# Branch gate a's weight units spread between those of queries and recurrence input; gates kept as sums, their tanh taken in place beside gate b

## The chip, the cores and the metric

The kernel runs on one core of a Trainium2 chip. The metric is the device time of one launch in microseconds (us). TensorE multiplies matrices out of SBUF into PSUM, VectorE (DVE) and ScalarE (ACT) work on tiles of 128 partitions, and SyncE (SP) issues nearly all the transfers from HBM. Each engine works through its own instructions in the order that the program fixed; engines wait for one another through semaphores.

## The reference

One layer over a sequence of 256 positions of width 2048, one core, float32:

```python
h = _modulate(_rms_norm(x, norm1_g), shift1, scale1)
proj = jnp.einsum("bsd,de->bse", h, w_in)
lru_x, lru_gate, q, k, v, g_a, g_b = jnp.split(proj, split_idx, axis=-1)
rec = _rg_lru(causal_conv(lru_x), ...)
y_a = (rec * gelu(lru_gate)) @ w_lru_out
y_b = _swa_sink_attention(q, k, v, ...) @ w_attn_out
merged = sigmoid(g_a) * y_a + sigmoid(g_b) * y_b
x = x + gate1 * (merged @ w_out)
x = x + gate2 * (relu(h2 @ w_ff1) ** 2 @ w_ff2)      # h2 from the second norm
```

The six vectors shift1 to gate2 are `silu(c) @ w_ada + b_ada`. The sigmoids of both branch gates are computed as tanh of half the argument; the 1 that belongs to it is added where the gate is multiplied, and a half later on.

## The kernel before

Everything is kept transposed: 128 features on the partitions, 256 positions in a row. A block of 128 output features is called f. The input projection has 84 blocks: 2 of keys, 2 of values, 16 of queries, 16 of recurrence input (`lx`), 16 of the gelu gate (`lg`), 16 of gate a (`F_GA`), 16 of gate b (`F_GB`).

Each weight and each activation is split into a high part and a rest, and three products are summed. For weights ScalarE writes the high part `wh` (L161) and DVE the rest `wl` (L163), 1024 columns at a time, each with four buffers (`WH_BUFS`). The raw weights come into four buffers of 1 MB (`RAW_BUFS`), which the loads of `w_ada` use too: `ada_unit` loads 1 MB and DVE multiplies it with the broadcast condition and sums it up (L287, 96 times in all). This text calls that a wada sum.

Work is cut into units of one weight load each. A wide unit (`gemm_wide`) has all 16 row blocks of one f: 32 matmuls, 2 splits of 1024 columns on each engine, and at the end ScalarE copies one half of the PSUM tile out (L197) and DVE adds the other half (L198). The blocks up to f = 55 were begun in earlier passes; their remaining row blocks make narrow units (`gemm`): two f of 6 row blocks each (1536 weight columns) for keys to the first four gelu gates, one f of 10 row blocks (1280 columns) for the other gelu gates and the first four blocks of gate a. So gate a has 4 narrow units and 12 wide ones, gate b 16 wide ones.

The list `units` sets the order: keys, values, 8 units of queries, 8 of recurrence input, 14 of the gelu gate, 16 of gate a, 16 of gate b, and then 48 wide units for the projections of the two branches and of the merged branches (`ya_unit`, `yb_unit`, `out_unit`), and the MLP. Behind each unit a credit, in proportion to its columns, takes steps from the list `side` that earlier units put there with `later`: attention scores and values, the recurrence (convolution L566 and L568, gates L576 to L582, decay, scan), the gelu. A second credit issues wada sums. A scheduler then settles each engine's order. `ya_unit(0)` first splits the 16 recurrence outputs into high part and rest (L146, L147).

Activation functions that need a table loaded into ScalarE go through `table`, which keeps functions of one table together; the tanh of the branch gates (L637, L640) before the change does not go through it.

Of the kernel before, what the change touches and what calls it, by code (L numbers as in the profile page):

```python
# [12 lines left out]
AF = mybir.ActivationFunctionType  # L13
# [13 lines left out]
F_K, F_V, F_Q, F_LX, F_LG, F_GA, F_GB = 0, 2, 4, 20, 36, 52, 68  # L27
# [31 lines left out]
def hybrid_layer(ctx: ExitStack, tc: tile.TileContext, x, xt, wada, w_p, w_r, w_f, vec, lruw, relb,  # L59
# [19 lines left out]
    def pair(dt=F32):  # L79
        return kp.tile([P, 2, T], dt, tag="k2", name=nm("k"))  # L80
# [101 lines left out]
    def gemm_wide(parts, acts, join=True, out=None):  # L182

        ps = pg.tile([P, 2, T], F32, tag="pg", name=nm("pg"))
        n = len(acts)
        for k, hl in enumerate(acts):
            wh, wl = parts[k * P // WCH]
            w = slice(k * P % WCH, k * P % WCH + P)
            if k > 0:
                te.matmul(ps[:, 0], lhsT=wl[:, w], rhs=hl[:, 0], start=False, stop=False)  # L190
            te.matmul(ps, lhsT=wh[:, w], rhs=hl, start=k == 0, stop=k == n - 1)  # L191
            if k == 0:
                te.matmul(ps[:, 0], lhsT=wl[:, w], rhs=hl[:, 0], start=False, stop=False)  # L193
        if not join:
            return ps
        t = tmp([P, T]) if out is None else out
        se.activation(t, ps[:, 1], AF.Copy)  # L197
        ve.tensor_tensor(out=t, in0=ps[:, 0], in1=t, op=ALU.add)  # L198
        return t
# [91 lines left out]
    h = [None] * KT  # L291
# [71 lines left out]
    res = {}  # L363
# [45 lines left out]
    def add_unit(run, src=None, n=2048, native=False):  # L409
        if src is None:  # L410
            src = w_f[full[0]]
            full[0] += 1
        units.append((run, src, n, native))

    def later(cost, fn, *a):
        side.append((cost, fn, a))

    def in_unit(f, fin, nf=1):

        kd = _done(f)  # L420
        if kd:
            n = (KT - kd) * nf * P
            src = w_r[w_off[0]:w_off[0] + n * P].rearrange("(p n) -> p n", p=P)
            w_off[0] += n * P

            def run(w):
                for i in range(nf):
                    o = i * (KT - kd)
                    ps = gemm_native(w, o, kd, KT) if f in NATIVE_REST else gemm(w, o, h[kd:])
                    fin(f + i, ps, res[f + i])  # L430
            add_unit(run, src, n, f in NATIVE_REST)
        else:
            add_unit(lambda w: fin(f, gemm_wide(w, h), None))

    def in_units(f0, n, fin):
        f = f0
        while f < f0 + n:
            nf = 2 if f + 1 < f0 + n and _done(f) == _done(f + 1) and _done(f) >= KT // 2 else 1
            in_unit(f, lambda f, ps, part: fin(f - f0, ps, part), nf)
            f += nf  # L440
# [186 lines left out]
        ve.tensor_tensor(out=part, in0=ps, in1=part, op=ALU.add)  # L627
        later(1.6, lru_gelu, j)

    bg = [None]  # L630

    def branch_gate(f, ps, part):
        if part is None:
            if f % 2 == 0:
                bg[0] = pair()
            res[f] = bg[0][:, f % 2]
            se.activation(res[f], ps, AF.Tanh, scale=0.5)  # L637
        else:
            ve.tensor_tensor(out=part, in0=ps, in1=part, op=ALU.add)
            se.activation(part, part, AF.Tanh, scale=0.5)  # L640


    att, mg = {}, {}
# [129 lines left out]
            ada_unit()  # L773


    in_units(F_K, 2, k_fin)
    in_units(F_V, 2, v_fin)
    in_units(F_Q, 16, q_fin)
    in_units(F_LX, 16, lx_fin)
    in_units(F_LG, 16, lg_fin)  # L780
    in_units(F_GA, 16, lambda f, ps, part: branch_gate(F_GA + f, ps, part))
    in_units(F_GB, 16, lambda f, ps, part: branch_gate(F_GB + f, ps, part))
    n_ya = len(units)
    n_z = n_ya + 32 + Z_FROM
    n_ff1 = n_ya + 48
# [152 lines left out]
```

## Time and profile before

| | |
|---|---|
| median of 3 runs | 1588.1 us (1587.84 to 1588.21) |
| the profiled execution | 1587.3 us, of which the span from the first to the last instruction is 1585.5 us |
| TensorE busy | 1546.4 us (98% of the span) |
| VectorE busy | 1217.3 us (77%) |
| ScalarE busy | 886.7 us (56%) |
| matmuls in the records | 9812 |

A profile shows one execution. Busy time is the union of the instructions' records on an engine; a wait is idle time before an instruction, put down to whatever released it last. PE is TensorE, PEld its weight loads. "L163" is line 163 of the kernel, `x16` a count, "PEclk" the granted clock of TensorE as a share of its upper level.

### The profile page before, as it was taken

The page shows a single profiled execution, that of the slowest core. Times are in us where ns is not written, and L with a number is a line of the kernel's source. Part 1 is how long each engine was busy: PE and PEld are TensorE (multiplying, and loading weights), DVE is VectorE, ACT ScalarE, POOL GpSimd, SP SyncE. Part 2 cuts the span into 40 slices and gives each one's busy share as a digit, 9 for nine tenths or more (in the row PEclk, how much of TensorE's full clock was granted, in tenths as well). Part 3 has the DMA queues.
Part 4 walks back from the last instruction along what each step waited for, and adds up shares of the span by engine and source line. Part 5 has one row for each costly group of instructions (what it writes and reads, how often), then busy time and mean ns, then how long its engine had stood idle before and what let it go on. Part 6 is the DMA issues. An engine that isn't in the chain of part 4 may idle for free.

```text
span 1585.5 us, 24919 instructions
## 1 busy us (share of the span) xinstructions
PE 1546.4 (98%) x9812; PEld 1385.7 (87%) x9812; DVE 1217.3 (77%) x1941; ACT 886.7 (56%) x1510; POOL 0.2 (0%) x4
## 2 busy tenths in 40 slices
PE   4999999999999999999999999999999999999997
PEld 3999998899988888888889988888888888888886
DVE  5898998898999878788898877965665556655664
ACT  5733447686796564445455863356434663356553
POOL 0000000000000000000000000000000000000000
PEclk6999999999999999999999999999999999999999
DMA  7998986556867768777886666965555555555551
GB/s 304 355 336 322 351 286 213 187 191 235 299 242 273 286 249 305 278 293 291 325 305 228 241 247 241 349 240 186 186 186 186 188 188 190 192 190 191 189 187 54
DMA packets 61125, 387.89 MB, mean 245 GB/s; under 512 B 6512, under 2 KB 10960, under 8 KB 18640
## 3 DMA queue, kind: packets, MB, share of 16 engines
q1 hardware_dynamic: 55728, 380.66, 66.2%
q10 hardware_dynamic: 5280, 5.64, 1.1%
q8 instruction: 77, 1.26, 0.3%
q14 instruction: 40, 0.33, 0.1%
HBM read 384.13 MB, written 2.15 MB: 244 GB/s over the span
## 4 chain that ended last, share of the span: by engine, by line
PE 90%; DVE 5%; issue 2%; ACT 2%; DMA 2%; ACTq 0%; DVEq 0%
PE pg L191 45%; PE pg L190 21%; PE pg L179 5%; PE pg L178 5%; PE pg L177 5%; PE pg L206 2%; DVE wl L163 2%; PE pg L193 1%; DMA ra<-in_wada_dram 1%; PE pg L726 1%; PE pg L727 1%; PE pg L728 1%; DVE t L500 1%; DVE t L527 1%; PE pa L532 1%
## 5 line engine op out<-in xcount | busy, mean ns | idle before, releaser
L191 PE MATMUL pg<-k,wh 128*128 128x512 f32 x3120 | 1078.0, 395 | 1.1 <-DVE k L147 1.1
L163 DVE TENSOR_TENSOR wl<-rw,wh 128x1024 fp32r<-128x1024 f32 (+2 forms) x534 | 627.2, 1179 | 267.4 <-ACT wh L161 261.2
L190 PE MATMUL pg<-k,wl 128*128 128x256 f32 x2925 | 818.1, 280 | 0.0
L161 ACT ACTIVATE wh<-rw 128x1024 fp32r<-128x1024 f32 (+2 forms) x534 | 541.1, 1020 | 493.2 <-PE pg L191 328.1
L191 PEld LDWEIGHTS pg<-k,wh 128*128 128x128 f32 x3120 | 572.2, 188 | 120.6 <-issue 1.4
L190 PEld LDWEIGHTS pg<-k,wl 128*128 128x128 f32 x2925 | 550.9, 188 | 9.5 <-ACT k L146 0.5
L177 PE MATMUL pg<-k,wh 128*128 128x256 f32 x832 | 238.1, 288 | 6.7 <-ACT k L146 6.5
L179 PE MATMUL pg<-k,wl 128*128 128x256 f32 x832 | 234.1, 284 | 4.1 <-DVE wl L163 4.1
L178 PE MATMUL pg<-k,wh 128*128 128x256 f32 x832 | 236.4, 285 | 0.1
L287 DVE CUSTOM_DVE_ANT_0 ra<-ra,scr,vc 128x2048 f32<-128x2048 f32 x96 | 225.1, 2346 | 11.7 <-DMA ra<-in_wada_dram 11.6
L177 PEld LDWEIGHTS pg<-k,wh 128*128 128x128 f32 x832 | 158.0, 190 | 9.7 <-ACT k L146 7.3
L179 PEld LDWEIGHTS pg<-k,wl 128*128 128x128 f32 x832 | 158.3, 191 | 5.6 <-DVE wl L163 5.3
L178 PEld LDWEIGHTS pg<-k,wh 128*128 128x128 f32 x832 | 158.7, 191 | 1.2 <-issue 0.5
L754 DVE SCALAR_TENSOR_TENSOR k<-pg,mod,k 128x256 f32<-128x256 f32 x128 | 61.9, 483 | 34.5 <-PE pg L191 32.4
L743 ACT ACTIVATE t<-t 128x256 f32<-128x256 f32 x55 | 23.0, 418 | 70.5 <-DVE t L198 70.4
L198 DVE TENSOR_TENSOR t<-pg,t 128x256 f32<-128x256 f32 x131 | 54.7, 418 | 0.3 <-ACT t L197 0.3
L193 PE MATMUL pg<-k,wl 128*128 128x256 f32 x195 | 54.5, 279 | 0.0
L197 ACT ACTIVATE t<-pg 128x256 f32<-128x256 f32 x131 | 48.0, 366 | 0.3 <-PE pg L191 0.3
L193 PEld LDWEIGHTS pg<-k,wl 128*128 128x128 f32 x195 | 36.7, 188 | 8.5
L727 PE MATMUL pg<-z,wh 128*128 128x256 f32 x144 | 41.0, 285 | 0.0
L728 PE MATMUL pg<-z,wl 128*128 128x258 f32 x144 | 40.8, 284 | 0.0
L726 PE MATMUL pg<-z,wh 128*128 128x258 f32 x144 | 40.8, 283 | 0.0
(161 smaller groups left out, 961.4 us busy)
## 6 DMA issues: line engine op xcount, KB each, us to landing
rw<-in_w_f_dram SPq DMA_DIRECT2D x204, 1024.0 KB, 4.9
ra<-in_wada_dram SPq DMA_DIRECT2D x96, 1024.0 KB, 6.3
rw<-in_w_p_dram SPq DMA_DIRECT2D x31, 1024.0 KB, 7.1
rw<-in_w_r_dram SPq DMA_DIRECT2D x20, 768.0 KB, 4.5
rw<-in_w_r_dram SPq DMA_DIRECT2D x16, 640.0 KB, 3.9
bt<-ud ACTq DMA_DIRECT2D x8, 512.0 KB, 3.8
lw<-in_lruw_dram SPq DMA_DIRECT2D x4, 512.0 KB, 5.0
k<-in_x_dram SPq DMA_DIRECT2D x8, 256.0 KB, 5.5
```

The lines of the kernel that those rows point to most:

```text
L161: pin(se.activation(wh[:, :c], raw[:, o:o + c], AF.Copy))
L163: pin(ve.tensor_tensor(out=wl[:, :c], in0=raw[:, o:o + c], in1=wh[:, :c].bitcast(F32), op=ALU.subtract))
L177: te.matmul(ps, lhsT=wh[:, w], rhs=hl[:, 0], start=k == 0, stop=False)
L178: te.matmul(ps, lhsT=wh[:, w], rhs=hl[:, 1], start=False, stop=False)
L179: te.matmul(ps, lhsT=wl[:, w], rhs=hl[:, 0], start=False, stop=k == n - 1)
L190: te.matmul(ps[:, 0], lhsT=wl[:, w], rhs=hl[:, 0], start=False, stop=False)
L191: te.matmul(ps, lhsT=wh[:, w], rhs=hl, start=k == 0, stop=k == n - 1)
L193: te.matmul(ps[:, 0], lhsT=wl[:, w], rhs=hl[:, 0], start=False, stop=False)
L287: pin(ve.tensor_tensor_reduce(out=raw, in0=raw, in1=scr, scale=1.0, scalar=vc[:, V_BADA + c:V_BADA + c + 1], op0=ALU.mult, op1=ALU.add, ac ...
L726: te.matmul(ps, lhsT=wh[:, e], rhs=z[k][:, 0:258], start=k == 0, stop=False)
L727: te.matmul(ps[:, 0:256], lhsT=wh[:, e], rhs=z[k][:, 258:514], start=False, stop=False)
L754: ve.scalar_tensor_tensor(out=x1[f], in0=ps[:, i], scalar=mod[:, 5 * KT + f:5 * KT + f + 1], in1=x1[f], op0=ALU.mult, op1=ALU.add)
```

## The change

`in_units` and `add_unit` still give each unit its part of the weight array, in the same order as before, so no address changes. The list of units is then put together in another order: keys and values, then the 16 units of queries and recurrence input with the 12 wide units of gate a spread among them (three behind every four), then the 14 gelu-gate units, the four narrow units of gate a, and gate b.

`gemm_wide` writes a gate's sum (L197, L198) straight into the tile in which the gate is kept (`gate_slot`) instead of into a temporary tile. The tanh is taken in place later: each unit of gate b puts two steps of 0.4 into `side`, one for the gate-a block of the same number and one for its own, and both now go through `table` with the exponential's table.

```diff
-            add_unit(lambda w: fin(f, gemm_wide(w, h), None))
+            add_unit(lambda w: fin(f, gemm_wide(w, h, out=gate_slot(f)), None))
...
+    bg = {}
+    def gate_slot(f):
+        if f // 2 not in bg:
+            bg[f // 2] = pair()
+        res[f] = bg[f // 2][:, f % 2]
+        return res[f]
+    def gate_tanh(f):
+        table("exp", se.activation(res[f], res[f], AF.Tanh, scale=0.5))
     def branch_gate(f, ps, part):
-        if part is None:
-            if f % 2 == 0:
-                bg[0] = pair()
-            res[f] = bg[0][:, f % 2]
-            se.activation(res[f], ps, AF.Tanh, scale=0.5)
-        else:
+        if part is not None:
             ve.tensor_tensor(out=part, in0=ps, in1=part, op=ALU.add)
-            se.activation(part, part, AF.Tanh, scale=0.5)
+        if f >= F_GB:
+            later(0.4, gate_tanh, f - F_GB + F_GA)
+            later(0.4, gate_tanh, f)
...
+    def of(f0, n, fin):
+        start = len(units)
+        in_units(f0, n, fin)
+        new = units[start:]
+        del units[start:]
+        return new
+    def spread(main, extra):
+        done = 0
+        for i, u in enumerate(main):
+            units.append(u)
+            while done < len(extra) * (i + 1) // len(main):
+                units.append(extra[done])
+                done += 1
+    u_k, u_v = of(F_K, 2, k_fin), of(F_V, 2, v_fin)
+    u_q, u_lx, u_lg = of(F_Q, 16, q_fin), of(F_LX, 16, lx_fin), of(F_LG, 16, lg_fin)
+    u_ga = of(F_GA, 16, lambda f, ps, part: branch_gate(F_GA + f, ps, part))
+    u_gb = of(F_GB, 16, lambda f, ps, part: branch_gate(F_GB + f, ps, part))
+    units += u_k + u_v
+    spread(u_q + u_lx, u_ga[4:])
+    units += u_lg + u_ga[:4] + u_gb
```

What this does to the order on the engines is shown at three places. In the changed kernel's rows the lines of the old tanh, L637 and L640, have become L640 alone, and later lines stand 8 to 24 further on.

First place, DVE in the stretch of gelu-gate units. `ra` is the tile of a `w_ada` load, `rw` a raw weight tile, `wl` a rest. A load takes the raw buffer that came free first. Before, the load `ra_4639` gets the buffer of `rw_4421`, whose last reader is the first row:

```order
L163 TENSOR_TENSOR wl_4429<-rw_4421,wh_4427 128x256
L582 TENSOR_TENSOR k_507<-t_4467,t_4311 128x256
L582 TENSOR_TENSOR k_524<-t_4475,t_4362 128x256
L627 TENSOR_TENSOR k_708<-pg_4492,k_708 128x256
L163 TENSOR_TENSOR wl_4486<-rw_4482,wh_4484 128x1024
L163 TENSOR_TENSOR wl_4490<-rw_4482,wh_4488 128x256
L582 TENSOR_TENSOR k_524<-t_4528,t_4362 128x256
L287 ISA ra_4639,mod<-ra_4639,scr,vc 128x2048
```

In the changed kernel the wada sum with the fewest rows between its buffer's last reader and itself, within the gelu-gate units, is this one (`ra_5119`, in the buffer of `rw_4922`):

```order
L163 TENSOR_TENSOR wl_4930<-rw_4922,wh_4928 128x256
L589 SCALAR_TENSOR_TENSOR t_4837<-t_4837 128x256
L589 SCALAR_TENSOR_TENSOR t_4849<-t_4849 128x256
L589 SCALAR_TENSOR_TENSOR t_4907<-t_4907 128x256
L591 SCALAR_TENSOR_TENSOR t_4837<-t_4837 128x256
L591 SCALAR_TENSOR_TENSOR t_4849<-t_4849 128x256
L627 TENSOR_TENSOR k_674<-pg_4984,k_674 128x256
L163 TENSOR_TENSOR wl_4978<-rw_4974,wh_4976 128x1024
L163 TENSOR_TENSOR wl_4982<-rw_4974,wh_4980 128x256
L591 SCALAR_TENSOR_TENSOR t_4907<-t_4907 128x256
L589 SCALAR_TENSOR_TENSOR t_4915<-t_4915 128x256
L287 ISA ra_5119,mod<-ra_5119,scr,vc 128x2048
```

Six rows stood between before, ten stand there now, with one weight split of each width in both.

Second place, ACT where gate a and the recurrence's last steps of a group of four meet. Before, the gates' tanh (L637) alternates with the square root (L596), and each change loads a table:

```order
L596 ACT_TABLE_LOAD
L596 ACTIVATE t_4885<-t_4885 128x256
L161 ACTIVATE wh_5122<-rw_5120 128x1024
L637 ACT_TABLE_LOAD
L637 ACTIVATE k_5105<-t_5102 128x256
...
L596 ACT_TABLE_LOAD
L596 ACTIVATE t_4940<-t_4940 128x256
L637 ACT_TABLE_LOAD
L637 ACTIVATE k_5105<-t_5163 128x256
L596 ACT_TABLE_LOAD
L596 ACTIVATE t_4991<-t_4991 128x256
```

In the changed kernel the tanh of gate a (L640) stands behind the last group's square roots, among the tanh of the gelu (L622), under one table load:

```order
L622 ACT_TABLE_LOAD
L622 ACTIVATE t_5680<-t_5680 128x256
...
L640 ACTIVATE k_794<-k_794 128x256 x2
L640 ACTIVATE k_2785<-k_2785 128x256 x2
L161 ACTIVATE wh_5688<-rw_5686 128x1024
L161 ACTIVATE wh_5692<-rw_5686 128x1024
L620 ACTIVATE t_6055<-k_708 128x256
L640 ACTIVATE k_811<-k_811 128x256 x2
L640 ACTIVATE k_3147<-k_3147 128x256 x2
```

In all, ACT's order has 22 table loads before and 17 now.

Third place, DVE ahead of `ya_unit(0)`, where the recurrence outputs are split (L147). Before, a wada sum and a weight split stand between the last gate-b sums and the first of them:

```order
L163 TENSOR_TENSOR wl_6537<-rw_6529,wh_6535 128x1024
L198 TENSOR_TENSOR t_6572<-pg_6539,t_6572 128x256
L287 ISA ra_6725,mod<-ra_6725,scr,vc 128x2048
L163 TENSOR_TENSOR wl_6584<-rw_6580,wh_6582 128x1024
L147 TENSOR_TENSOR k_6637<-k_460,k_6637 128x256
L147 TENSOR_TENSOR k_6640<-k_460,k_6640 128x256
L147 TENSOR_TENSOR k_6643<-k_477,k_6643 128x256
```

In the changed kernel the wada sum stands elsewhere, and five splits of recurrence outputs come ahead of the next weight split:

```order
L163 TENSOR_TENSOR wl_6503<-rw_6495,wh_6501 128x1024
L198 TENSOR_TENSOR k_6505<-pg_6506,k_6505 128x256
L147 TENSOR_TENSOR k_6609<-k_460,k_6609 128x256
L147 TENSOR_TENSOR k_6612<-k_460,k_6612 128x256
L147 TENSOR_TENSOR k_6615<-k_477,k_6615 128x256
L147 TENSOR_TENSOR k_6618<-k_477,k_6618 128x256
L147 TENSOR_TENSOR k_6621<-k_507,k_6621 128x256
L163 TENSOR_TENSOR wl_6554<-rw_6550,wh_6552 128x1024
```

The first split of a recurrence output has moved from three rows behind the last gate sum of that stretch to the row right behind it.

## Rows read from the trace of the kernel before

**Rows 1.** Span and mean granted TensorE clock of the core; and a line of the page's first part: busy us, share of the span, instructions.

```profile
core 0: 1585.5 us, clock 0.990
...
PE 1546.4 (98%) x9812; PEld 1385.7 (87%) x9812; DVE 1217.3 (77%) x1941; ACT 886.7 (56%) x1510; POOL 0.2 (0%) x4
```

**Rows 2.** TensorE's waits over the whole run: line that waited, what released it: us in total, times, longest.

```profile
PE pg L179 <- DVE wl L163: 4.1, 4, 2.1
PE pa L532 <- DVE as L500: 2.1, 5, 0.9
PE pa L458 <- DVE t L455: 1.1, 1, 1.1
PE pg L191 <- DVE k L147: 1.1, 1, 1.1
PE pa L576 <- ACT k L637: 0.4, 1, 0.4
```

**Rows 3.** Stretches: queries and recurrence input (230 to 345 us), gelu gate and narrow units of gate a (345 to 421), wide gate units (421 to 583), the table changes of the second place above (440 to 480), and one stretch of narrow units alone (160 to 200) and of wide ones alone (600 to 640). Columns: us, busy us (xinstructions) of PE, PEld, DVE, ACT, POOL, then granted clock, DMA share, GB/s.

```profile
230.00:345.00 115.00, 110.12 (x923) 96.69 (x922) 101.06 (x329) 81.58 (x236) 0.00 (x0) 1.00 0.57 194
345.00:421.00 76.00, 73.92 (x586) 72.88 (x586) 69.06 (x127) 54.75 (x98) 0.00 (x0) 0.98 0.71 244
421.00:583.00 162.00, 161.25 (x921) 140.74 (x919) 142.52 (x210) 117.67 (x205) 0.00 (x0) 1.00 0.75 274
160.00:200.00 40.00, 40.00 (x342) 40.00 (x341) 39.15 (x59) 17.23 (x20) 0.00 (x0) 1.00 0.95 348
600.00:640.00 40.00, 40.00 (x231) 35.04 (x231) 35.52 (x50) 18.62 (x27) 0.00 (x0) 1.00 0.82 301
...
440.00:480.00 40.00, 39.49 (x221) 34.21 (x220) 37.06 (x61) 37.29 (x65) 0.00 (x0) 1.00 0.68 242
```

**Rows 4.** The longest of TensorE's waits behind a weight split, in order of time (start us, us, engine, instruction): SP's issue of the load, DVE's rows, then TensorE's last matmul before the wait and the first behind it.

```profile
376.62 0.33 SPq L272 DMA_DIRECT2D ra<-in_wada_dram  x1
...
378.36 0.42 DVE L627 TENSOR_TENSOR k<-pg,k 128x256 f32<-128x256 f32 x1 [1.10 <-PE pg L179]
378.70 1.55 DVE L163 TENSOR_TENSOR wl<-rw,wh 128x1024 fp32r<-128x1024 f32 x2
380.17 0.42 DVE L582 TENSOR_TENSOR k<-t,t 128x256 f32<-128x256 f32 x1
383.96 2.35 DVE L287 CUSTOM_DVE_ANT_0 ra<-ra,scr,vc 128x2048 f32<-128x2048 f32 x1 [3.37 <-DMA ra<-in_wada_dram]
386.24 0.42 DVE L589 SCALAR_TENSOR_TENSOR t<-t 128x256 f32<-128x256 f32 x1
386.58 0.42 DVE L627 TENSOR_TENSOR k<-pg,k 128x256 f32<-128x256 f32 x1
387.30 1.22 DVE L163 TENSOR_TENSOR wl<-rw,wh 128x1024 fp32r<-128x1024 f32 x1
...
386.22 0.28 PE L178 MATMUL pg<-k,wh 128*128 128x256 f32 x1
388.57 0.39 PE L179 MATMUL pg<-k,wl 128*128 128x256 f32 x1 [2.08 <-DVE wl L163]
```

**Rows 5.** Stretches right behind that wait, same columns as rows 3.

```profile
389.80:393.20 3.40, 3.40 (x18) 3.40 (x18) 3.40 (x9) 3.37 (x8) 0.00 (x0) 0.50 0.85 294
393.20:397.00 3.80, 3.80 (x34) 3.80 (x33) 3.55 (x8) 3.67 (x9) 0.00 (x0) 1.00 0.69 226
```

**Rows 6.** The other wait of that kind, on DVE and on TensorE.

```profile
265.25 2.35 DVE L287 CUSTOM_DVE_ANT_0 ra<-ra,scr,vc 128x2048 f32<-128x2048 f32 x1 [1.45 <-DMA ra<-in_wada_dram]
...
271.51 0.39 PE L179 MATMUL pg<-k,wl 128*128 128x256 f32 x1 [1.26 <-DVE wl L163]
```

**Rows 7.** The wait ahead of `ya_unit(0)`: DVE's rows, then TensorE's.

```profile
579.51 0.42 DVE L198 TENSOR_TENSOR t<-pg,t 128x256 f32<-128x256 f32 x1
579.85 2.35 DVE L287 CUSTOM_DVE_ANT_0 ra<-ra,scr,vc 128x2048 f32<-128x2048 f32 x1
582.12 1.22 DVE L163 TENSOR_TENSOR wl<-rw,wh 128x1024 fp32r<-128x1024 f32 x1
583.25 1.09 DVE L147 TENSOR_TENSOR k<-k,k 128x256 fp32r<-128x256 f32 x3
...
583.82 0.47 PE L191 MATMUL pg<-k,wh 128*128 128x512 f32 x1 [1.06 <-DVE k L147]
```

**Rows 8.** ScalarE's groups by line and shape: count, busy us, mean ns of one, idle before them: the gates' tanh and their table loads.

```profile
L637 ACT ACTIVATE k<-t 128x256 f32<-128x256 f32 x28 | 11.7, 416 | 23.1 <-DVE t L198 23.1
L637 ACT ACT_TABLE_LOAD x4 | 5.1, 1283 | 0.1
```

**Rows 9.** DVE's groups by line and shape, same columns: the weight splits, the wada sum, a step of the convolution, the scan.

```profile
L163 DVE TENSOR_TENSOR wl<-rw,wh 128x1024 fp32r<-128x1024 f32 x498 | 608.2, 1223 | 267.4 <-ACT wh L161 261.2
L287 DVE CUSTOM_DVE_ANT_0 ra<-ra,scr,vc 128x2048 f32<-128x2048 f32 x96 | 225.1, 2346 | 11.7 <-DMA ra<-in_wada_dram 11.6
L568 DVE SCALAR_TENSOR_TENSOR t<-k,vc,t 128x255 f32<-128x255 f32 x16 | 7.7, 479 | 0.1
L598 DVE TENSOR_TENSOR_SCAN k<-t,k 128x256 f32<-128x256 f32 x16 | 10.8, 683 | 0.1
```

**Rows 10.** The page's line on the loads of `w_ada`: count, KB each, median us from issue to landing.

```profile
ra<-in_wada_dram SPq DMA_DIRECT2D x96, 1024.0 KB, 6.3
```

## Prediction before the run

> **What bounds the kernel now.** I read the spans and busy times first [rows 1]: TensorE is busy 1546.4 of 1585.5 us. Then the windows [rows 3]. 342 narrow matmuls fill 40 us with no idle time, and so do 231 wide ones, which is 40/231 x 32 = 5.54 us for a wide unit. So TensorE runs at its own pace wherever it is fed; the change alters no matmul, and all it can win is time in which TensorE stands or runs slowly. The windows also say where that is: 4.9 us idle in the stretch of queries and recurrence input, 2.1 in the gelu-gate and narrow stretch, 0.8 in the 162 us of gate units. The first two are also where VectorE is densest, 101.06/110.12 = 0.92 and 69.06/73.92 = 0.93 of TensorE's busy time; among the wide gate units it is 0.88.
>
> TensorE's waits [rows 2] name the stops. L179 waits for a rest of a weight four times. Two of them lie in the part that is reordered: 2.08 us at 388.57 [rows 4] and 1.26 us at 271.51 [rows 6]. L576 waits 0.4 us for a gate's tanh on ScalarE, L191 1.06 us ahead of `ya_unit(0)` [rows 7], and L532 five times for 2.1 us in the attention.
>
> The longest stop shows the mechanism [rows 4]. The `w_ada` load takes the raw buffer that came free first, so SP can issue it only at 376.62, when that buffer's last split is done. DVE gets to the wada sum with little work between, waits 3.37 us for the data, needs 2.3 us for the sum itself, and the next weight split starts at 387.30. TensorE has used up the splits made ahead and stands from 386.50 to 388.57. Behind it the granted clock is 0.50, the lower level of 1.2 GHz, for 3.4 us, after an idle stretch of TensorE; then it is 1.00 again [rows 5]. In those 3.4 us there are 18 matmuls; at the 342 per 40 us of [rows 3] it would be 29, so 11 x 0.117 = 1.3 us is lost by count, and 3.4/2 = 1.7 by the clock. I take 1.7 since the records may miss some matmuls. The stop costs 2.08 + 1.7 = 3.75 us in all.
>
> **The change, part by part.** I count the rows of the two orders and price DVE's from the trace. A row's price is the time until the next can start, which is 0.08 us less than its duration (in [rows 4] a row of 0.42 us starts 0.34 before the next): 1.14 us for a split of 1024 columns, 2.26 for a wada sum, 0.39 for a step of the convolution, 0.60 for a scan [rows 9], 0.34 for anything of 256 columns.
>
> *Queries and recurrence input.* Twelve wide units come in: 12 x 5.54 = 66.5 us for TensorE, and for DVE 62.6 us: 24 splits (27.4), 5 wada sums (11.3), 10 unit sums (3.4), and 20.5 us of recurrence and attention steps that the credit now takes earlier. The ratio becomes 163.7/176.6 = 0.93, where it was 0.92. The stretch isn't thinned out, since DVE's steps follow their units' columns. What gets better is the bunching. The largest run of DVE work ahead of TensorE, summed over a few units, falls from 7.6 to 4.9 us.
>
> *Gelu gate and the narrow units of gate a.* The splits are the same. One wada sum more (+2.26), seven convolution steps fewer (-2.73), two scans more (+1.20), four other rows more (+1.36): DVE gets 2.1 us more for the same 73.9 us of TensorE. So this stretch stays as tight as it is, and its stop goes only if the late load there is gone.
>
> *Where the loads' leads stand.* I call lead the DVE work between the last split that reads the buffer and the wada sum. Before, it is 1.14 + 5 x 0.34 = 2.8 us at the longest stop, to which a 1.10 us wait of DVE adds [rows 4]; the load landed 7.3 us after its issue, where the median is 6.3 [rows 10]. The other leads in the narrow units are 4.8, 4.9 and 8.0, without a wait of DVE. At the earlier stop it is 1.4. After, the narrow stretch has 6.8, 4.2, 7.8, 4.3 and 9.1 us: 4.2 = 1.14 + 9 x 0.34 is the place shown in the order. Among queries and recurrence input it has 5.3, 3.9, 2.8, 0.2 and 3.9 to 15. The 0.2 is worse than any before; the rows ahead of it wait some 4 us for ScalarE's exponentials, by the attention's chain, and I count that as lead.
>
> *What is won.* Stop at 271.51: 1.26. Stop at 388.57: 2.08, and 1.7 for the clock behind it. L576: 0.4, since its tanh no longer shares ScalarE with a unit's table changes. L191: 1.06, since the first split of a recurrence output now stands right behind the last gate sum, with no 2.26 us wada sum and 1.14 us weight split between [rows 7]. Sum: 6.5.
>
> *What may come in.* A lead of 4.2 against a median landing of 6.3 makes DVE wait 2.1 us, 1.3 less than the 3.37 of the longest stop, so TensorE's wait would be 2.08 - 1.3 = 0.8; with leads of 4.8 nothing was lost. Three places are of this kind (4.2, 4.3, and 0.2 with its cover). Bounds: nothing, and one full repeat of 3.75 us. I take half, 1.9, since two of the leads are nearer to 4.8 (no wait) than to 2.8. The attention's waits on L532 I leave at 2.1 us; they could vanish or double.
>
> *Tanh later and in place.* The same number of tanh of 0.416 us [rows 8], now behind gate b's units; nobody but the later merging reads them. The sums go straight into kept tiles, which a gelu's last product must have freed. That product precedes by units, so I cost it at nothing; if it is late, the copy at a unit's end waits, and the nearest row for such a wait is the 1.06 of [rows 7]. The order has 22 table loads before and 17 after, each 1.283 us of ScalarE with 0.1 us of idle time before four of them [rows 8]. ScalarE is busy 37.29 of 40 us where the gates' tanh alternates with the square roots, yet TensorE does 39.49 of 40 there [rows 3]: at most 0.5 us is on the path, and I count none beyond L576. SP's loads follow the new order of units and are 96 wada loads still [rows 10]; the DMA share, 0.57 and 0.75 in the two stretches that are mixed [rows 3], leaves room.
>
> The Trainium skill, "ScalarE: Activation LUTs", section "What ACT_TABLE_LOAD costs", puts a switch at about 1283 ns for the load and 1380 ns of drain. The trace agrees on 1283 and shows no idle time like the second; by the page five switches would be 13.3 us of ScalarE.
>
> **Sum.** -6.5 + 1.9 = -4.6 us. The profiled execution took 1587.3 us (span 1585.5), 0.8 below the median of the runs, so the median goes from 1588.1 to 1583.5. Best of this case: no new wait and no L532 wait, -8.6, 1579.5. Worst: a full repeat and L532's waits doubled, -6.5 + 3.75 + 2.1 = -0.65, 1587.4.
>
> **Rivals.**
> *The stops only move.* The narrow stretch has 2.1 us more DVE work and the attention has a load with a lead of 0.2. One or two full repeats of [rows 4] and the attention's waits as they are: 1588.1 - 6.5 + 3.75 or 7.5 = 1585.4 to 1589.1. For it speaks that DVE's ratio stays at 0.92 to 0.93 in both stretches; against it that fewer leads are short than before.
> *Slower, by late loads in the narrow units.* A stop there is followed by a wait of the next load's buffer too, since each split that is late frees its buffer late. With 3.75 each, the kernel is slower by more than can be told from no change (0.2%, 3.2 us) from the third stop on: (6.5 + 3.2)/3.75 = 2.6. Three give 1588.1 - 6.5 + 11.25 = 1592.9. For it: six wada sums in 76 us instead of five. Against it: leads above 4.8 never stopped anything.
> *Table loads are on the path.* Then five of them give 6.4 us more: 1583.5 - 6.4 = 1577.1. Against it stands the 0.5 us of [rows 3].
>
> **How the numbers follow.** The likeliest case gets 0.64, its own range 1579.5 to 1587.4; three quarters of it lie below 1584.9, where the 0.2% ends. The moved stops get 0.20, all within 0.2%; slower 0.13; the tables 0.03. Faster: 0.48 + 0.03 = 0.51. Same: 0.16 + 0.20 = 0.36. Slower: 0.13. The range takes in the likeliest case and the moved stops with some margin for the copy that waits, 1579.0 to 1590.5.
>
> **What would show it.** Right: the waits list has no L179 behind L163 with a DVE wait for `w_ada` ahead of it among the gelu-gate units, and after the start no stretch of half clock; no L576 wait on a gate's tanh, no L191 wait before `ya_unit(0)`; 17 table loads. TensorE's idle time between 230 and 585 us falls from some 9 to some 4 or 5 us. Wrong: L287 waits of 2 us or more in either dense stretch with TensorE idle within 5 us behind them, or another half-clock stretch; a copy L197 that waits for a kept tile. What I can foresee least is whether a load lands in 5 or in 8 us at the places where the lead is about 4; the time hangs on that.

## The result

The changed kernel is slower: 1594.8 us median of 7 runs (1591.2 to 1595.4) against 1588.1 us (1587.8 to 1589.9). The ratio is 1.0038, with a 95% interval of 1.0029 to 1.0048, so 4.6 to 7.6 us. The forecast was 1583.5 us, with a range up to 1590.5.

The span and busy line after, to be read beside [rows 1], and TensorE's waits beside [rows 2]:

```profile
core 0: 1593.0 us, clock 0.994
...
PE 1551.1 (97%) x9812; PEld 1388.5 (87%) x9812; DVE 1217.7 (76%) x1941; ACT 880.5 (55%) x1505; POOL 0.2 (0%) x4
```

```profile
PE pa L532 <- DVE t L527: 3.7, 2, 2.2
PE pa L532 <- DVE as L500: 2.0, 3, 1.0
PE pg L179 <- DVE wl L163: 1.6, 3, 0.8
PE pa L576 <- DVE t L568: 1.4, 1, 1.4
PE pa L458 <- DVE t L455: 1.1, 1, 1.1
PE pg L191 <- ACT wh L161: 1.0, 1, 1.0
...
PE pa L576 <- ACT t L581: 0.6, 1, 0.6
```

Everything that the forecast said would go has gone: L179's 1.26 and 2.08 us in the reordered part, L576 behind a gate's tanh, L191 behind L147. New are two waits of L532 for L527 (the attention's normalised weights), two of L576 (for the convolution and for L581), and a pair of stops at 494 us. TensorE is busy for 4.7 us more with the same matmuls. Two stretches run at half clock, where before there is one [rows 5]; that makes 1.7 us of the 4.7, and no single row names the rest. The two stretches stand here with the attention's stretch of both kernels, from the first matmul of the queries to the last of the attention (columns as in rows 3; before, then after):

```profile
232.20:329.20 97.00, 93.21 (x795) 80.52 (x794) 83.51 (x292) 67.76 (x213) 0.00 (x0) 1.00 0.59 200
```

```profile
232.80:349.20 116.40, 110.44 (x822) 92.37 (x821) 91.25 (x293) 74.04 (x220) 0.00 (x0) 0.99 0.58 201
...
251.60:255.00 3.40, 3.40 (x18) 3.40 (x18) 3.40 (x9) 3.39 (x16) 0.00 (x0) 0.50 0.71 202
497.40:500.80 3.40, 3.40 (x18) 3.40 (x18) 2.94 (x5) 1.64 (x5) 0.00 (x0) 0.50 0.97 390
```

At 0.50 each of the two loses 1.7 us by the clock. The row to look at is VectorE's in the attention: 91.25 of 116.4 us, 0.83 of TensorE's busy time, where before it was 83.51 of 97.0, or 0.90. VectorE is less busy, and TensorE waits for it more. What VectorE waited for in the same stretches, before and after:

```profile
DVE ra L287 <- DMA ra<-in_wada_dram: 3.0, 2, 1.5
```

```profile
DVE ra L287 <- DMA ra<-in_wada_dram: 8.5, 4, 3.1
DVE as L512 <- ACT t L510: 6.6, 2, 3.5
...
DVE t L500 <- DMA bt<-ud: 0.8, 1, 0.8
```

These are its waits for the `w_ada` load, the exponentials on ScalarE, and the tile of position biases (`bt`, 512 KB, one buffer, issued from ScalarE's own queue). Together they are 15.9 us, where before there are 3.0. (Its waits for TensorE itself and for ScalarE's weight splits are left out, and 1.7 us for the convolution's first step in the kernel before.)

The first new stop, in order of time on DVE and then on TensorE:

```profile
245.90 2.35 DVE L287 CUSTOM_DVE_ANT_0 ra<-ra,scr,vc 128x2048 f32<-128x2048 f32 x1 [1.99 <-DMA ra<-in_wada_dram]
...
248.50 0.16 DVE L512 TENSOR_TENSOR as<-as 128x8 f32<-128x8 f32 x1
...
250.68 0.48 DVE L500 CUSTOM_DVE_ANT_0 t<-pa,bt,vc 128x256 f32<-128x256 f32 x1
251.08 0.28 DVE L527 TENSOR_SCALAR t<-t,as 128x128 f32<-128x128 f32 x1
```

```profile
248.91 0.28 PE L178 MATMUL pg<-k,wh 128*128 128x256 f32 x1
251.42 0.33 PE L532 MATMUL pa<-idt,t 128*128 128x128 f32 x1 [2.23 <-DVE t L527]
```

ScalarE's last exponential of this group ended at 246.4, but the short step that uses it (L512) and the next group's scores (L500) are queued on DVE behind a wada sum that waited for its load. TensorE's next instruction is the transpose (L532) of what L527 makes.

The second stop behind L527 is built in the same way, and its wada sum is the one with the lead of 0.2 us:

```profile
303.05 0.17 DVE L512 TENSOR_TENSOR as<-as 128x8 f32<-128x8 f32 x1 [3.14 <-ACT t L510]
...
306.48 2.35 DVE L287 CUSTOM_DVE_ANT_0 ra<-ra,scr,vc 128x2048 f32<-128x2048 f32 x1 [3.02 <-DMA ra<-in_wada_dram]
...
311.46 0.28 DVE L527 TENSOR_SCALAR t<-t,as 128x128 f32<-128x128 f32 x1
```

```profile
311.80 0.33 PE L532 MATMUL pa<-idt,t 128*128 128x128 f32 x1 [1.45 <-DVE t L527]
```

The longest of the load waits, 3.15 us at 284 us, costs nothing that shows: TensorE has no wait there until 296 us.

### The profile page after: what moved, and what is told of

It reads as the page before. It is cut to its first block, busy times and chain, and to the rows that moved or that the text cites. A ratio compares the mean times of both kernels' runs of the same rounds, so it can differ in the third digit from the quotient of the medians.

```text
span 1593.0 us, 24928 instructions
## 1 busy us (share of the span) xinstructions
PE 1551.1 (97%) x9812; PEld 1388.5 (87%) x9812; DVE 1217.7 (76%) x1941; ACT 880.5 (55%) x1505; POOL 0.2 (0%) x4
## 3 DMA queue, kind: packets, MB, share of 16 engines
q8 instruction: 77, 1.26, 0.3%
## 4 chain that ended last, share of the span: by engine, by line
PE 89%; DVE 5%; DMA 2%; issue 2%; ACT 1%; ACTq 0%; DVEq 0%
PE pg L191 44%; PE pg L190 21%; PE pg L179 5%; PE pg L178 5%; PE pg L177 5%; DMA ra<-in_wada_dram 2%; PE pg L206 2%; DVE wl L163 2%; PE pg L193 1%; PE pg L736 1%; PE pg L734 1%; PE pg L735 1%; PE pa L539 1%; PE pa L532 1%; DVE ra L287 1%
## 5 line engine op out<-in xcount | busy, mean ns | idle before, releaser
L191 PE MATMUL pg<-k,wh 128*128 128x512 f32 x3120 | 1081.1, 395 | 1.0 <-ACT wh L161 1.0
L191 PEld LDWEIGHTS pg<-k,wh 128*128 128x128 f32 x3120 | 573.6, 188 | 121.2 <-ACT wh L161 1.2
L287 DVE CUSTOM_DVE_ANT_0 ra<-ra,scr,vc 128x2048 f32<-128x2048 f32 x96 | 225.1, 2345 | 17.3 <-DMA ra<-in_wada_dram 17.1
L179 PE MATMUL pg<-k,wl 128*128 128x256 f32 x832 | 234.8, 285 | 1.6 <-DVE wl L163 1.6
L179 PEld LDWEIGHTS pg<-k,wl 128*128 128x128 f32 x832 | 158.9, 192 | 2.9 <-DVE wl L163 2.7
L193 PE MATMUL pg<-k,wl 128*128 128x256 f32 x195 | 54.9, 282 | 0.0
L193 PEld LDWEIGHTS pg<-k,wl 128*128 128x128 f32 x195 | 36.6, 188 | 8.1 <-issue 0.3
L198 DVE TENSOR_TENSOR t<-pg,t 128x256 f32<-128x256 f32 x103 | 42.9, 417 | 0.3 <-ACT t L197 0.3
L197 ACT ACTIVATE t<-pg 128x256 f32<-128x256 f32 x103 | 37.5, 364 | 0.3 <-PE pg L191 0.3
```

Source lines behind the costliest of these rows:

```text
L179: te.matmul(ps, lhsT=wl[:, w], rhs=hl[:, 0], start=False, stop=k == n - 1)
L287: pin(ve.tensor_tensor_reduce(out=raw, in0=raw, in1=scr, scale=1.0, scalar=vc[:, V_BADA + c:V_BADA + c + 1], op0=ALU.mult, op1=ALU.add, ac ...
```

## How the kernels are compared

One stretch holds the same matmuls in both orders: from the first matmul of the queries to the first of `ya_unit(0)`. Both times were read from TensorE's timeline, its rows matched with the program's order. For "above its own time" the matmuls of a stretch were priced at 0.2335 us for 512 columns, 0.118 for 256, a fitted price for the small ones and 0.135 for each change from weight products to small matmuls. The prices are a fit over the units of before, after, e1 and e2 that show no wait (scatter 0.19 us a unit); the fit sets only what counts as zero.

Ratios are to runs of the kernel before taken beside each kernel, whose medians lie between 1587.2 and 1588.9 us. A stretch is read from one profiled execution, and executions of one kernel differ (e20: 1588.7 to 1595.1 us). The profiled ones of e3, e14, e18 and e20 took 1.4 to 2.5 us more than their median, that of e10 4.4 us less. So stretches that differ by 2 us or less aren't told apart here.

| kernel | median us | ratio to before (95%) | stretch | attention above own time | rest above own time |
|---|---|---|---|---|---|
| before | 1588.1 | 1 | 351.6 | 0.2 | 4.1 |
| changed | 1594.8 | 1.0038 (1.0029 to 1.0048) | 357.7 | 5.8 | 5.1 |
| e1 order only | 1593.7 | 1.0038 (1.0025 to 1.0050) | 355.9 | 2.9 | 5.5 |
| e2 gates only | 1586.5 | 0.9993 (0.9984 to 1.0002) | 349.0 | 0.3 | 1.5 |
| e3 changed, sums rest in the attention | 1593.4 | 1.0036 (1.0023 to 1.0050) | 353.7 | 2.2 | 4.4 |
| e4 and in the narrow units | 1610.9 | 1.0147 (1.0133 to 1.0161) | 348.5 | 1.8 | -0.4 |
| e6 before, sums rest as in e4 | 1590.0 | 1.0011 (1.0002 to 1.0020) | 348.2 | -0.8 | 2.3 |
| e7 block behind | 1588.0 | 1.0005 (0.9996 to 1.0014) | 351.7 | 0.7 | 3.9 |
| e8 block ahead | 1606.7 | 1.0121 (1.0107 to 1.0135) | 372.3 | -0.7 | 23.2 |
| e9 gates only, sums rest in the narrow units | 1582.8 | 0.9969 (0.9957 to 0.9980) | 346.6 | 0.2 | -0.8 |
| e10 spread among queries | 1605.2 | 1.0115 (1.0099 to 1.0130) | 364.3 | 1.2 | 16.6 |
| e11 spread among recurrence input | 1587.9 | 1.0006 (0.9996 to 1.0015) | 350.8 | 1.3 | 2.5 |
| e12 changed, loads ahead | 1595.6 | 1.0060 (1.0048 to 1.0073) | 358.8 | 8.4 | 3.2 |
| e13 gates only, loads ahead | 1587.5 | 1.0002 (0.9993 to 1.0011) | not read | | |
| e14, e15 changed, sums shifted | 1596.8, 1598.4 | 1.0049, 1.0063 | 359.5, 357.6 | 6.5, 8.0 | 5.4, 2.1 |
| e18, e19 gates only, sums shifted | 1588.8, 1588.4 | 1.0004, 1.0002 | 349.7, 349.1 | 1.8, 0.9 | 0.6, 1.2 |
| e20 changed, one bias tile | 1592.6 | 1.0024 (1.0013 to 1.0034) | 357.1 | 4.7 | 5.6 |
| e21 is e15, one bias tile | 1590.8 | 1.0009 (0.9999 to 1.0020) | 352.5 | 2.5 | 2.3 |

## The experiments

### The two halves of the change: e1 and e2

e1 takes the gates of before into the new order:

```diff
-            add_unit(lambda w: fin(f, gemm_wide(w, h, out=gate_slot(f)), None))
+            add_unit(lambda w: fin(f, gemm_wide(w, h), None))
...
+            se.activation(res[f], ps, AF.Tanh, scale=0.5)
```

> The spread order of units, with the gates as they were: sums in a temporary tile, tanh at the unit. Theory W (a late w_ada load holds DVE, and the attention steps queued behind the wada sum come late): the place of the loads in the attention stays about as in the changed kernel, so the two waits of L532 for L527 (2.23 and 1.45 us) and the half clock behind the first stay, 1591 to 1596 us. Theory T (what costs is the tanh put off into gate b, which bunches with the recurrence's last steps and makes the stop at 494 us, 1.85 us of waits and some 2 us of half clock): that stop is gone, so about 4 us less than the changed kernel, 1591 us or below. By both the tables go back towards 22.

e2 is the converse: the changed gates, with `in_units` called in the old order.

> The old order of units, with gates kept as sums and their tanh taken beside gate b. Theory W: nothing is added to the attention, which comes before every gate; the longest stop of before (L179 at 388 us, 3.75 us with its clock) stays or shifts by a row or two, L576 behind the gate's tanh (0.4 us) goes: 1586 to 1589 us. Theory T: the tanh beside gate b makes a stop of some 4 us: 1591 to 1593 us.

The order alone carries the loss (+6.1 us of the medians), and the gates alone can't be told from no change (-1.1). Theory T falls: a tanh put off costs nothing. e2's stretch is 2.6 us shorter than before, 1.5 of which are the waits of L576 (0.4) and L191 (1.06) that are gone. Its L179 wait at 387 us is still there, 2.28 us, as expected, but no half clock follows it. In e1, L532's wait for L527 is 1.9 us, and there is no half clock either; the stop at 494 us is there in another form (L179 1.18 and L193 1.28 us behind weight splits). So e1 loses the half of what the changed kernel loses in the attention, and as much behind it.

### Resting the wada sums: e3, e4, e6, e9

e3, e4 and e6 differ in the range alone (`n_q`: first unit of queries; `n_gb`: first of gate b):

```diff
-        if n < n_ya:
+        if n_q <= n < n_gb:
+            pass
+        elif n < n_ya:
             ada_credit += size / 2048 * ADA_RATE
```

> The changed kernel, in which the credit for wada sums rests during the units of queries, recurrence input and the spread gate units; the sums left over are taken beside the projection of the recurrence branch, where VectorE is least busy. Theory W: DVE's three waits there for w_ada (1.99, 3.15, 3.02 us) go, and with them L532's waits for L527 (3.7 us in two) and the half clock of 251 to 255 us (2 us): 1588 to 1590 us, with the stop at 494 us still there. Theory D (the attention's own steps are bunched behind wide units, whatever the loads do): the L532 waits stay within 1 us, 1593 to 1596 us.

> The same, with the credit resting until gate b begins, so over the gelu-gate units and the narrow units of gate a too. Theory W, widened to wada sums that stand ahead of something due (2.26 us on DVE even where the load is in time): the stops at 400 us (L576, 1.36) and 494 us (L179 0.85 and the half clock) go as well, L191's 1.0 behind ScalarE stays: 1584 to 1587 us. Theory T: the stop at 494 us stays, since ScalarE makes it: 1588 to 1591 us.

> The kernel before, with the credit for wada sums resting from the first unit of queries to the last narrow unit of gate a, as in e4 for the changed kernel. What is read is the stretch from the values' transposes to the first unit of the merged projection (541.6 us before, 548.6 changed, 539.4 in e4); the end pays for the sums that come late, as in e4, 1595 to 1612 us in all. Theory V (all the stops in both orders come from VectorE having too much to do ahead of TensorE, and a wada sum is the largest piece): without the sums the two orders are alike, 538 to 541 us. Theory I (the spread itself costs, by mixing wide units into the attention): the old order stays some 4 us or more ahead, 535 us or less.

> e2 (the old order, tanh put off) with the credit for wada sums resting over the gelu-gate units and the narrow units of gate a alone: five sums, taken later beside the branches' projections. Theory V: the stop of L179 at 387 us (2.28 us and 1.7 of half clock) goes, and five sums more beside 48 wide units cost nothing that shows: 1581 to 1584 us. Theory P (sums paid back late cost what they save, since the transfers beside the projections are at 80% and more): 1586 to 1590 us.

The totals of e3, e4 and e6 say little, since the sums come back where VectorE and the transfers are nearly full. In e4, from 590 to 850 us, beside the projections:

```profile
590.00:850.00 260.00, 255.24 (x1443) 219.78 (x1442) 250.09 (x339) 120.69 (x185) 0.00 (x0) 1.00 0.93 348
...
856.20 0.38 PE L193 MATMUL pg<-k,wl 128*128 128x256 f32 x1 [3.68 <-DVE wl L163]
```

VectorE is at 96% there, the transfers at 0.93 of their time, and TensorE loses 4.8 us, then stands 3.68 at once (2.85 us in e3 and 2.76 in e6 near the same place). The stretch ahead of it answers the question. With the sums resting in the attention (e3) the attention's loss falls from 5.8 to 2.2 us; with them resting in the narrow units too (e4) the rest goes from 5.1 to -0.4: the stops at 400 and 494 us are gone. So the wada sums are a condition of most of the loss. e4's and e6's stretches are alike within 0.4 us, as theory V had it, though not cleanly: e6 has a wait of 2.36 us at its end, ahead of `ya_unit(0)`, and its attention is 2.6 us better than e4's. That part is not the sums'.

The total that VectorE stands is not what sets the loss. In e4's attention it stands as long for exponentials and biases as in the changed kernel for loads, exponentials and biases (15.8 and 15.9 us), its share of TensorE's busy time is lower still (78.6 of 108.8 us, 0.72), and TensorE loses 1.8 us instead of 5.8:

```profile
DVE as L512 <- ACT t L510: 12.6, 5, 3.9
...
DVE t L500 <- DMA bt<-ud: 3.2, 2, 2.2
```

What e4 lacks is a wada sum, with its load, between the exponentials' end and the weights.

e9 rests five sums alone, in the old order with the new gates, and pays them back where there is room (transfers at 0.85 from 590 to 850 us). It is the fastest of all, 5.4 us under before. Its narrow stretch, beside the second row of [rows 3], is full:

```profile
345.00:421.00 76.00, 76.00 (x614) 74.86 (x613) 62.99 (x124) 58.02 (x104) 0.00 (x0) 1.00 0.61 209
```

Theory P falls for five sums. For ten or more most of what is saved is lost again: e3's median is 1.4 us under the changed kernel, while its stretch is 4.0 shorter.

### Where the wide units stand: e7, e8, e10, e11

```diff
-    spread(u_q + u_lx, u_ga[4:])
+    units += u_q + u_lx + u_ga[4:]         # e7
+    units += u_ga[4:] + u_q + u_lx         # e8
+    spread(u_q, u_ga[4:]); units += u_lx   # e10
+    units += u_q; spread(u_lx, u_ga[4:])   # e11
```

> The changed kernel with the twelve wide units of gate a in one block behind the recurrence input, ahead of the gelu gate. Theory I: the attention sees no wide unit, its losses go (about 5 us of the changed kernel's), 1588 to 1590 us. Theory V: the attention is as it was before, and the recurrence's steps now fall beside wide units instead of narrow ones, so the narrow gelu-gate units have less beside them: 1584 to 1588 us. A theory that the narrow units lose wherever they are placed last (the stop where narrow units end and gate b begins) expects 1591 to 1594.

> The changed kernel with the twelve wide units in one block ahead of the queries, where nothing of the attention or the recurrence is there yet. Theory I and theory V: queries to narrow gate a run as in the old order with the tanh put off (e2), 1585 to 1588 us. If wide units among attention and recurrence had been worth something in themselves (relief for VectorE), it is lost here and e8 is above e7 by 2 us or more.

> The changed kernel with all twelve wide units spread among the 8 units of queries, and the recurrence input behind them unmixed. The stretch from the first query matmul to the first of the recurrence projection is read: 351.6 us before, 357.7 changed, 351.7 with the block behind. Theory M (attention steps beside wide units lose time, the more of them the more): 356 to 359 us, the time 1592 to 1596 us. Theory C (which w_ada load meets which attention step is chance of the order): no relation to the number of wide units, 350 to 360 us.

> The changed kernel with the twelve wide units spread among the 8 units of recurrence input, the queries ahead unmixed. Theory M: the attention's first groups run as before, the later ones lose, so about half of the changed kernel's loss: 354 to 356 us in the stretch, 1590 to 1592 us in all. Theory C: as in e10, no relation.

In one block behind (e7), or spread among the recurrence input alone (e11), the wide units can't be told from the kernel before; against e2, which has the same gates, e7's stretch is 2.7 us longer and e11's 1.8. e7's 1588.0 us lies where theories I and V meet and doesn't part them. e8 and e10 failed as tests of the totals, for a cause that the prediction had named and costed at nothing. TensorE in e8, its last matmul and the next:

```profile
514.12 0.59 PE L577 MATMUL pa<-t,lw 128*128 128x256 f32 x2
531.98 0.77 PE L191 MATMUL pg<-k,wh 128*128 128x512 f32 x1 [17.26 <-DVE k L198]
```

A unit's sum goes into a kept tile, and by then all kept tiles are taken; the rows of DVE just ahead of that L198 are the gelu's last products (L623, L624), which free them and which were still to be taken from `side`. The wait is 17.26 us (10.16 in e10), and the clock is at its lower level from 517.2 to 537.6 us. The changed kernel shows no such wait. e10's attention alone still speaks. Of the wide units, 2.4 fall into the attention's stretch in e11, 6.0 in the changed kernel and 11.2 in e10; the losses are 1.3, 5.8 and 1.2 us. Theory M, in the form "the more of them the more", falls. e11's stretch (350.8 us) is under the 354 to 356 that M gave it, but with so few wide units in the attention it says little of them.

e10 also shows that load waits alone are not the cost. VectorE's waits for `w_ada` in its attention are as long as the changed kernel's 8.5 us, while those for the exponentials are 1.4 us instead of 6.6:

```profile
DVE ra L287 <- DMA ra<-in_wada_dram: 8.4, 5, 2.4
```

### Late loads: e12 and e13

```diff
             ada_unit()
             ada_credit -= 1
+        if n_q <= n < n_gb and not ada_raw:
+            ada_dma()
```

> The changed kernel, in which from queries to narrow gate a one w_ada load is always issued a sum ahead, so that it holds a raw buffer longer; no sum is left out or moved to another unit. Theory L (the wait for the load is what costs: DVE's 1.99, 3.15, 3.02 and 1.85 us): those waits go, and with them L532's waits for L527 and the half clock behind them, 1587 to 1590 us, near what resting the sums gave in that stretch (348.6 us). Theory S (the sum's own 2.3 us on VectorE is enough): the stops stay, 1592 to 1596 us. Where the raw buffer that is held makes a weight late, TensorE or ScalarE waits for a weight's load instead, and the time is above 1596 us.

> e2 (old order, tanh put off) with the same loads ahead. Theory L: L179 at 271 us (1.5 us) and at 387 us (2.28 us and its clock) go: 1581 to 1584 us, as with the resting sums of e9. Theory S: 1585 to 1588 us.

e12 settles nothing between L and S, because the edit didn't do what it was for:

```profile
DVE ra L287 <- DMA ra<-in_wada_dram: 16.8, 13, 3.9
```

The changed kernel has 17.1 us of this wait in the whole run. A load asked for earlier still needs one of the four raw buffers; that they are what is short is likely, but no run shows it. e13 is 1587.5 us, 1.0 above e2 and not under it, inside the range of theory S. In e18 and e19 this wait is 25.3 and 20.2 us in the whole run, more than in the changed kernel, and TensorE loses little. A DVE that waits for `w_ada` is not by itself what TensorE loses. A kernel with the sums in place and their loads in time was not obtained, so these two runs don't part L from S.

### Is it chance? e14, e15, e18, e19

The same two orders with the credit for sums 0.33 and 0.66 lower at the first unit of queries:

```diff
+        if n == n_q:
+            ada_credit -= 0.33
```

> The changed kernel, in which the credit for wada sums starts a third of a sum lower at the first unit of queries, so that the same number of sums falls into slightly later units. Read is the stretch from the first query matmul to the first of the recurrence projection (357.7 us changed, 349.0 in e2 with the old order). Theory C (the loss is which sum meets which attention step in this one order): the stretch moves by some 3 us or more, and with e15 the three shifts of the changed kernel overlap those of the old order. Theory M (the order with wide units among queries and recurrence input loses by itself): 355 to 360 us whatever the shift.

> The same with two thirds of a sum. Theory C: a third value, anywhere from 349 to 360 us. Theory M: 355 to 360 us.

> e2 (the old order with the gates as sums and the tanh put off), with the same shift by a third of a sum. Theory M: 348 to 352 us in the stretch, clearly under the changed kernel at every shift. Theory C: it scatters as the spread order does, up to 355 us or more.

> e2 with the shift by two thirds of a sum. Theory M: 348 to 352 us. Theory C: scatter, as above.

The spread order takes 357.6 to 359.5 us in the stretch at three shifts, the old order 349.0 to 349.7. Theory C falls for this order: it loses 8 to 10 us to the old one wherever the sums are. The medians agree: 7.8, 7.9 and 10.0 us between the two orders, each against its own runs of before. What changes with the shift is which wait does it. VectorE's waits for `w_ada` in the attention are 8.5 us in the changed kernel, 0.8 in e14 and 0.9 in e15, and the loss is no smaller there. So late `w_ada` loads are not needed for it. In e15 it is the bias, on ScalarE's queue, DVE and TensorE:

```profile
301.14 0.37 ACTq L481 DMA_DIRECT2D bt<-ud  x1
...
301.44 1.46 DVE L527 TENSOR_SCALAR t<-t,as 128x128 f32<-128x128 f32 x6
308.76 0.35 DVE L500 CUSTOM_DVE_ANT_0 t<-pa,bt,vc 128x128 f32<-128x128 f32 x1 [5.86 <-DMA bt<-ud]
...
309.57 0.69 PE L532 MATMUL pa<-idt,t 128*128 128x128 f32 x2 [4.69 <-DVE as L500]
```

The load lands 7.6 us after its issue, and DVE stands 5.86 us with nothing else in its order that it could do. The tile had been free since 293.7, when the previous group's last score step (L500) ended; the issue stands in ScalarE's order, behind that group's exponentials and some copies, and goes out 7.4 us later. Issuing it from another queue was not tried. The weights that L532 transposes (L527) are there from 302.9. The row that releases L532 is L500, which reads the next group's scores out of PSUM; scores and transposes share four PSUM tiles (`pa`). In e14 the longest stop stands behind the bias too, on DVE and on TensorE:

```profile
248.60 0.35 DVE L500 CUSTOM_DVE_ANT_0 t<-pa,bt,vc 128x128 f32<-128x128 f32 x1 [3.91 <-DMA bt<-ud]
...
251.79 0.48 PE L532 MATMUL pa<-idt,t 128*128 128x128 f32 x1 [3.49 <-DVE t L527]
```

### The bias load: e20 and e21

```diff
-        bt = sp.tile([P, 4, T], F32, tag="bias", name=nm("bt"), bufs=1)
-        se.dma_start(out=bt, ...)
+        if g == 0:
+            bias[0] = sp.tile([P, 4, T], F32, tag="bias", name=nm("bt"), bufs=1)
+            se.dma_start(out=bias[0], ...)
+        bt = bias[0]
```

> The changed kernel, in which the attention's bias tile is loaded for the first group alone and used for all eight (the other groups' scores get the wrong heads' bias; the work on them is the same). Seven loads of 512 KB and the waits on them are gone. Theory B (the bias load, issued late from ScalarE's queue into one tile, makes the attention late): the stretch of the attention comes down to within 2 us of its matmuls' own time (5.8 us above it in the changed kernel, 0.2 before), 1589 to 1592 us. Theory X (the steps meet wide units' splits and wada sums on VectorE, and the exponentials ScalarE's splits, whatever the bias does): 4 us or more above it, 1593 to 1597 us.

> The same on e15, where VectorE waited longest for the bias (6.7 us in two, and TensorE's wait of 4.69 us at 305 us behind the second). Theory B: that stop and the half clock behind it go, the attention's stretch from 8.0 us above its matmuls' time to 2 or less, 1590 to 1593 us. Theory X: still 4 us or more above, 1595 us or more.

In e21 the stop and its half clock are gone: 8.0 becomes 2.5 us, and the median falls by 7.6 us to what can't be told from before. So theory B holds in e15, where the bias is what DVE waits for. e20 settles less. Its median, 1592.6 us, lies between the two forecasts and 2.2 us under the changed kernel. In its profiled execution, the longest of its ten, the attention's loss goes from 5.8 to 4.7 only, by theory X; the stop at 250 us is still there (1.80 us, ahead of the same transposes) behind the normalised weights and a wada sum that waited 1.58 us for its load. So in the changed kernel the bias is not what makes its longest stop; whether it makes a part of the loss is open.

## Why the prediction was wrong

*What bounds it* held: TensorE is full wherever it is fed, and only stops and half clock moved the time. *What is won* held to the item: the two L179 waits, the half clock behind the second, L576's and L191's waits, 6.5 us, are all gone. Table loads are 17, and ScalarE's 6.4 us were worth nothing that can be told (e2), as counted.

*The step that failed is "queries and recurrence input"*, with its "largest run of DVE work falls from 7.6 to 4.9 us". It counted the work in DVE's order and no waiting. The work came out about as counted, 164.9 us for 163.7, from the first matmul of the queries to the first of the gelu gate:

```profile
232.80:427.40 194.60, 187.28 (x1348) 163.60 (x1348) 164.91 (x421) 133.74 (x322) 0.00 (x0) 0.99 0.60 210
```

But the ratio there is 0.88 and not 0.93, and in the attention 0.83, where DVE stood for 15.9 us on loads, exponentials and biases, 3.0 before. With it failed the sentence "the attention's waits on L532 I leave at 2.1 us; they could vanish or double": they are 5.7 us, and 1.7 us of half clock follow the longest. The 0.2 us lead with "some 4 us for ScalarE's exponentials, and I count that as lead" was a warning that I priced, with two leads of the narrow units, at half a stop. As lead it was 3.5 us (3.14 of it waiting), the load landed 6.5 us after its issue, and the place costs 1.45 us. Nor does the rule "with leads of 4.8 nothing was lost" hold: the longest stop stands behind a lead of 5.3 us, whose load took 7.3. In both places a wada sum and the next group's scores stand between the exponentials' end and the weights that TensorE needs; that is what the count of leads left out.

*The narrow stretch* "stays as tight as it is" held; that its stop would be gone did not help. Its stop moved to where narrow units meet gate b. ScalarE's split for the first wide unit of gate b starts only at 494.10, behind four rows of the gelu, and DVE's next split behind a wada sum (ScalarE, DVE, TensorE):

```profile
492.87 1.32 ACT L620 ACTIVATE t<-k 128x256 f32<-128x256 f32 x4
494.10 1.99 ACT L161 ACTIVATE wh<-rw 128x1024 fp32r<-128x1024 f32 x2
...
493.00 2.34 DVE L287 CUSTOM_DVE_ANT_0 ra<-ra,scr,vc 128x2048 f32<-128x2048 f32 x1
...
495.27 1.55 DVE L163 TENSOR_TENSOR wl<-rw,wh 128x1024 fp32r<-128x1024 f32 x2
...
495.19 0.50 PE L191 MATMUL pg<-k,wh 128*128 128x512 f32 x1 [1.00 <-ACT wh L161]
496.54 0.39 PE L179 MATMUL pg<-k,wl 128*128 128x256 f32 x1 [0.85 <-DVE wl L163]
```

This sum did not wait for its load: its 2.3 us are enough. With the half clock behind it the place costs 1.85 + 1.7 = 3.55 us, and the two new L576 waits 2.0.

*The sum as measured*: -6.5 for what is gone; +3.6 for L532 (5.7 instead of 2.1), +2.0 for L576, +1.85 at 494 us, +3.4 half clock in two windows. That is +4.35, and the stretch got 6.1 us longer: some 1.8 us lie in TensorE's busy time, and no row names them. *The slower rival* had the right sign and about the right time (1592.9), by stops behind late loads with half clock after them. But it put them in the narrow units, and had them come from leads of 4 us; the dear ones behind late loads are in the attention, where the lead alone is not what decides, and the one at 494 us has its load in time. That its time is near the measured one is therefore luck. *The kept tile* cost nothing, as said, in this order; e8 shows what it costs without its cover, 17 us instead of the 1.06 that I took from [rows 7].

**What is shown and what stays open.** Shown: the order carries the loss, not the gates; it does so at every shift of the sums tried; most of it goes when the wada sums rest there; the bias load makes most of the attention's loss in e15 (8.0 us with it, 2.5 without). Read from the traces, but not shown by an experiment: in the changed kernel it is a wada sum and its load behind the wait for the exponentials. Each of the two waits alone cost little, 8.4 us for loads in e10 and 12.6 us for exponentials in e4. Not settled: why the full spread loses in the attention when wide units among the queries alone (e10) hardly do, and whether a part of it (some 2 us, no more than stretches differ by) stays without sums. Each edit also lets the scheduler order other rows anew, so no experiment removed one wait and left all else in place.

## What to carry to other kernels

Count, ahead of an engine that works in order, not only its work but what it will wait for from outside (a load into a single buffer, another engine's results), and what stands behind that wait; an engine with a lower busy share can be the later one, and the total of its waits doesn't tell it either (e4). Spreading work evenly by columns does not spread a chain that goes through three engines and a load. When a background job's single step (here 2.3 us) is as long as the slack of the pipeline, the cheapest remedy may be to let it rest in the tight stretch, as long as the place where it is paid back has room on VectorE and in the transfers: five sums gained 3.8 us over e2, while of the 4.0 us that ten gained in e3's stretch 1.4 were left, and sixteen in e4 cost more than they gained.

## What the runs showed of the hardware

The granted clock does not follow the length of a stop alone. The 2.08 us stop of before is followed by 1.2 GHz [rows 4, 5]; a stop of 2.28 us at the same place in e2 is followed by no lower clock, nor is one of 1.9 us in e1 or one of 2.76 us at 850 us in e6 (each time 1.00 over the next 20 us). One of 1.80 us in e20 is followed by the lower level (0.51 from 252.2 to 255.7 us), and so are 1.00 and 0.85 us within 1.4 us at 494 us in the changed kernel.
